# adaLN in a two-layer diffusion block: the context vector's products on GpSimd and ScalarE

## The chip, the core and the metric

One core of a Trainium2 chip runs the kernel. The metric is device microseconds of one execution, the median over the runs shown. The engines' names in the rows are PE (TensorE, matmuls), PEld (its weight loads), DVE (VectorE), ACT (ScalarE), POOL (GpSimd) and SP (SyncE, which issues transfers).

## The reference, cut to what matters

Two layers over 256 latent tokens `h` and 256 context tokens `hc`, D = 1024. In each layer: a SwiGLU half step, token mixing by four kinds of attention, a second SwiGLU half step. Each sub-layer's input is normalised and modulated; shifts, scales and gates come from two conditioning vectors through one matrix per layer (adaLN):

```python
s_c, s_cc = silu(c), silu(c_ctx)
for l in range(2):
    mod   = (s_c  @ w_ada[l] + b_ada[l]).reshape(B, 9, 1, D)   # latent tokens
    mod_c = (s_cc @ w_ada[l] + b_ada[l]).reshape(9, D)         # context tokens
    h  = h  + 0.5 * mod[:, 2] * swiglu(modulate(h,  norm_ffn1[l], mod[:, 0], mod[:, 1]), ...)
    hc = hc + 0.5 * mod_c[2]  * swiglu(modulate(hc, norm_ffn1[l], mod_c[0],  mod_c[1]), ...)
    ...                                  # token mixing, modulations 3, 4, gate 5
    h  = h  + 0.5 * mod[:, 8] * swiglu(modulate(h, norm_ffn2[l], mod[:, 6], mod[:, 7]), ...)
    if not last:
        ...                              # the same for hc, with mod_c[5] to mod_c[8]
return rmsnorm(h, final_norm)
```

In layer 1, the last one, `mod_c[5]` to `mod_c[8]` have no use.

## The kernel before, in words

Activations lie feature-major in SBUF: 128 features on the partitions, up to 512 tokens (256 latent, 256 context) along the free axis. Products are made in split precision: each weight block of 128x1024 is loaded by SyncE (`wraw`, L124, three buffers), ScalarE makes its high part `whi` (L127) and VectorE the rest `wlo` (L128), with five buffers each; `mm3` (L132 on) then issues three matmuls for each of 8 contraction tiles.

A SwiGLU phase (`ffn`) walks over 22 feature tiles in three chunks of 8, 8 and 6. For each tile a **pair** of weights (gate and up) makes two accumulations in PSUM (`pgu`; the pool has four banks, that is two pairs), and `activate` forms the activation: `sg` = silu on ScalarE (L357), `af` on VectorE (L358), its high part `ah` on ScalarE (L371), the rest `al` on VectorE (L372). At a chunk's end come the **down** products `pd`: eight output tiles, each contracting over the 8 (or 6) activations of the chunk, and the residual's update on VectorE (L336).

The first pair of modulations of layer 0 is formed by matmuls in the opening. All others, 128 **tiles** of 128 output features, are spread over three SwiGLU phases by `Jobs`: 48 in layer 0's first (modulations 2 to 7), 32 in its second (8, and 0 to 2 of layer 1), 48 in layer 1's first (3 to 8). A pair counts as two slots and a down tile as one; the tiles are due at even steps over the first 56 slots, so a pair brings one or two in the phases with 48 tiles and one in the phase with 32. `ada_tile` has SyncE load a tile of the matrix (`wa`, L295, two buffers), and VectorE multiplies it with the latent and with the context vector, each product summed along the row (L298):

```python
for v in range(2):
    junk = pool.tile([P, D], F32, name="junk", tag="junk", bufs=1)
    ins = nc.vector.scalar_tensor_tensor(junk, w, 1.0, sbc[:, v], op0=ALU.mult, op1=ALU.mult, accum_out=m[:, t, v:v + 1])
```

After the eight tiles of a modulation `ada_end` adds the bias and folds in gain or factor (L305 to L310).

Each engine takes its instructions in a fixed order, which a scheduler derives from the program when it is built; transfers of weights and of `wa` tiles are issued by SyncE in one order, too. An instruction whose operands are late holds up everything behind it on its engine.

Of the kernel before, what the change touches and what calls it, by code (L numbers as in the profile page):

```python
# [11 lines left out]
F32 = mybir.dt.float32  # L12
F32R = mybir.dt.float32r
# [6 lines left out]
P = 128  # L20
D = 1024
# [16 lines left out]
# feature-major column tiles of w_in  # L38
# [11 lines left out]
def body(nc, tc, es, a):  # L50
# [9 lines left out]
    # ---------------------------------------------------------------- constants and small parameters  # L60
# [24 lines left out]
    rope = con[:, 0:4 * S].rearrange("p (a b) -> p a b", a=4)                 # cos32 sin32 cos64 sin64  # L85
    gmask = con[:, 4 * S:5 * S].rearrange("p (a b) -> p a b", a=2)
    nmask = con[:, 5 * S:6 * S]
    rev = pers.tile([P, P], F32R, name="rev")                                 # turns the 64 query columns of a grid row
# [9 lines left out]
    def late_constants():  # L98
        """-lam per layer, on every partition; rev"""
# [18 lines left out]
    # ---------------------------------------------------------------- helpers  # L118
    def weights(src, shape):
        """load a [128, k, cols] block of a weight and split it"""  # L120
# [19 lines left out]
    def rsqrt_cols(ps, n, inv, eps, eng):  # L140
        """[128, n] sums in PSUM -> 1 / sqrt(sum * inv + eps) in SBUF"""
# [16 lines left out]
    def rms_cols(parts, ntok, dim, eps, heads=1, eng=nc.gpsimd, pin=False):  # L158
        """parts [128, ntok]: squares that add up over the feature tiles. -> rstd [128 tokens, token tiles x heads]"""
# [10 lines left out]
    def rms_rows(y, ntok, heads=1, pin=False):  # L170
        """-> PSUM [128, ntok] with rstd of the tokens (and of the head of each partition) on every partition"""
# [10 lines left out]
    class Stats:  # L182
        """squares of the residual stream, summed tile by tile as it is finished"""
# [5 lines left out]
        def add(self, k, hv):  # L189
# [4 lines left out]
            if n == 0:  # L194
                nc.scalar.activation(acc, src, AF.Square)
            else:
                sq = tp.tile([P, S], F32, name="sq", tag="nt", bufs=3)
                nc.scalar.activation(sq, src, AF.Square)
                if n == KD - 1 and (len(self.n) == 1 or hv == CTX):        # the last tile's squares stay by themselves
                    self.parts[hv].append(sq)  # L200
                else:
                    nc.vector.tensor_add(acc, acc, sq)
# [5 lines left out]
    class Norm:  # L208
        """rmsnorm, scale and shift of the residual stream into the split operands u, half by half and tile by tile"""
# [23 lines left out]
        def rest(self, stats, hv, between, eng=nc.gpsimd, rs=None):  # L233
            """the norm of a half, with other work between its parts"""
# [12 lines left out]
    def finish_phase(tail, stats, halves, nxt):  # L247
        """the last feature tiles of a phase for one half after the other; the norm behind the first half is woven into the second"""
# [15 lines left out]
    def first_products(nrm, stats, halves, group, between=None):  # L264
        """the first products [(weights, PSUM, halves)] of a phase, k by k behind the norm; the norm of the second half is woven in"""
# [14 lines left out]
    # ---------------------------------------------------------------- adaLN  # L280
# [10 lines left out]

    def ada_tile(l, i, t, pool, sbc, pin):
# [3 lines left out]
        for v in range(2):  # L296
            junk = pool.tile([P, D], F32, name="junk", tag="junk", bufs=1)
            ins = nc.vector.scalar_tensor_tensor(junk, w, 1.0, sbc[:, v], op0=ALU.mult, op1=ALU.mult, accum_out=m[:, t, v:v + 1])  # L298
            if pin:
                tc.keep_in_program_order(ins)  # L300

    def ada_end(l, i):
        """+ bias; scale -> gain * (1 + scale); gate of a half step -> 0.5 * gate"""
# [11 lines left out]
    class Jobs:  # L315
        """adaLN tiles spread over the first slots of a phase of 64"""
# [30 lines left out]
    SKEW = 5                              # last feature tiles of a phase, done for one half after the other  # L347

    # ---------------------------------------------------------------- SwiGLU half step
    def ffn(l, nrm, stats, gate, wgu, wd, halves, nxt, jobs, fp, opening=None):  # L350
        ntok = S * len(halves)

        def activate(pg, pu, rs=None):
# [5 lines left out]
            else:  # L359
                # one PSUM tile per half: sums still without rstd, the shift's product behind them  # L360
# [72 lines left out]
    # ---------------------------------------------------------------- token mixing  # L433
# [3 lines left out]
    def mix(l, nrm, stats, gate, qh, nxt, mp):  # L437
        u = nrm.u
        nq = S * len(qh)                  # tokens that ask
# [15 lines left out]
        def proj(tile_id, ntok):  # L455
            """feature-major projection of u by one column tile of w_in -> PSUM"""
# [6 lines left out]
        def rotate(dst, src, which, rows=(0, P)):  # L463
            """dst[:, lat] = rope(src[:, lat]); both in SBUF, dst may be src"""
# [18 lines left out]
        def vtok(src_list, width):  # L483
            """token-major projection of u: src_list = blocks of k tiles [128, nk, width] -> PSUM per token tile"""
# [46 lines left out]
        # ---- q, k, v of the heads. Q[hd], K[hd]: lists of (stationary, moving) operands whose products add up to the scores  # L531
        Q, K, V = {}, {}, {}

        # MLA: the parts by themselves
        ML = {}

        class LatentNorm:
            """rmsnorm of a low-rank projection (its feature tiles in PSUM), split"""
# [60 lines left out]
        # differential: the blocks of 32 partitions hold pairs of parts (q, k) along the contraction; (hi, hi) lies where the projection left it  # L599
# [25 lines left out]
        def diff_v():  # L625
            """v of the differential heads and the rotary key that the MLA heads share"""
# [20 lines left out]
        # heads of 64: q = [hi lo] against k = [hi hi] and [lo lo]  # L647
# [49 lines left out]
        # neighbourhood bias and mask: the query columns lie reversed in it, the product with rev turns them  # L697
# [16 lines left out]
        # ---- softmax units  # L714
        ORD = (0, 2, 1, 3)                # order of the GQA heads
# [485 lines left out]
```

## Time and profile before

| | |
|---|---|
| median of 3 runs | 2155.68 us (2154.09 to 2156.24) |
| span of the profiled execution | 2153.2 us |
| TensorE busy | 2107.4 us, 98% |
| VectorE busy | 1469.2 us, 68% |
| ScalarE busy | 911.8 us, 42% |
| GpSimd busy | 180.7 us, 8% |
| the 256 adaLN products on VectorE | 312.3 us |

TensorE's matmuls overlap, so its busy time says that there is always one under way, not that each runs at its peak. Busy time of the other engines is a sum over stages; where one of them matters is told by the waits and by the timeline.

### The profile page before, as it was taken

The page shows a single profiled execution, that of the slowest core. Times are in us where ns is not written, and L with a number is a line of the kernel's source. Part 1 is how long each engine was busy: PE and PEld are TensorE (multiplying, and loading weights), DVE is VectorE, ACT ScalarE, POOL GpSimd, SP SyncE. Part 2 cuts the span into 40 slices and gives each one's busy share as a digit, 9 for nine tenths or more (in the row PEclk, how much of TensorE's full clock was granted, in tenths as well). Part 3 has the DMA queues.
Part 4 walks back from the last instruction along what each step waited for, and adds up shares of the span by engine and source line. Part 5 has one row for each costly group of instructions (what it writes and reads, how often), then busy time and mean ns, then how long its engine had stood idle before and what let it go on. Part 6 is the DMA issues. An engine that isn't in the chain of part 4 may idle for free.

```text
span 2153.2 us, 31572 instructions
## 1 busy us (share of the span) xinstructions
PE 2107.4 (98%) x12130; PEld 1805.8 (84%) x12130; DVE 1469.2 (68%) x2639; ACT 911.8 (42%) x1456; POOL 180.7 (8%) x322
## 2 busy tenths in 40 slices
PE   7999999999999999999999999999999999999998
PEld 5888888987777877988888898888889888999998
DVE  6776767678767665566665558767667887787655
ACT  3422222467655563432222233222225776765443
POOL 0000000110012112100000010000002433120000
PEclk9999999999999999999999999999999999999999
DMA  8555554241232223245444336555542335355553
GB/s 331 173 178 178 177 176 150 69 121 47 66 100 73 88 66 118 92 157 156 140 154 150 105 118 203 179 176 186 165 127 90 105 106 138 128 168 171 192 183 102
DMA packets 95207, 301.52 MB, mean 140 GB/s; under 512 B 18640, under 2 KB 20048, under 8 KB 94672
## 3 DMA queue, kind: packets, MB, share of 16 engines
q1 hardware_dynamic: 92080, 295.10, 43.0%
q0 software_dynamic: 2688, 4.20, 1.0%
q8 instruction: 96, 1.57, 0.3%
q14 instruction: 55, 0.45, 0.1%
q10 hardware_dynamic: 288, 0.20, 0.0%
HBM read 294.21 MB, written 1.05 MB: 137 GB/s over the span
## 4 chain that ended last, share of the span: by engine, by line
PE 89%; DVE 5%; ACT 2%; issue 1%; POOL 1%; DMA 1%; SPq 0%; DVEq 0%; POOLq 0%; ACTq 0%
PE pgu L134 13%; PE pgu L137 13%; PE pgu L138 13%; PE pd L137 6%; PE pd L138 6%; PE pd L134 6%; PE pgt L134 4%; PE pgt L137 4%; PE pgt L138 4%; PE av L789 2%; PE pj L134 2%; PE pj L137 2%; PE pj L138 2%; PE psS L735 2%; PE tps L775 1%
## 5 line engine op out<-in xcount | busy, mean ns | idle before, releaser
L127 ACT CAST whi<-wraw 128x1024 fp32r<-128x1024 f32 (+2 forms) x414 | 423.1, 1024 | 993.8 <-PE pgu L137 434.7
L128 DVE TENSOR_TENSOR wlo<-wraw,whi 128x1024 fp32r<-128x1024 f32 (+2 forms) x414 | 495.2, 1197 | 160.6 <-ACT whi L127 141.5
L134 PE MATMUL pgu<-uh,whi 128*128 128x512 f32 (+1 forms) x1440 | 511.9, 357 | 1.4 <-ACT sg L357 0.9
L137 PE MATMUL pgu<-ul,whi 128*128 128x512 f32 (+1 forms) x1440 | 512.7, 356 | 0.6 <-DVE ul L230 0.4
L138 PE MATMUL pgu<-uh,wlo 128*128 128x512 f32 (+1 forms) x1440 | 512.2, 356 | 0.0
L298 DVE SCALAR_TENSOR_TENSOR junk<-wa,sbc 128x1024 f32<-128x1024 f32 x256 | 312.3, 1220 | 3.1
L134 PEld LDWEIGHTS pgu<-uh,whi 128*128 128x128 f32 x1440 | 271.1, 189 | 43.4 <-issue 2.5
L137 PEld LDWEIGHTS pgu<-ul,whi 128*128 128x128 f32 x1440 | 272.1, 189 | 39.4 <-DVE ul L230 1.1
L138 PEld LDWEIGHTS pgu<-uh,wlo 128*128 128x128 f32 x1440 | 272.1, 189 | 39.1 <-DVE wlo L128 0.3
L137 PE MATMUL pd<-al,whi 128*128 128x512 f32 (+1 forms) x794 | 273.4, 344 | 0.2 <-DVE al L372 0.2
L134 PE MATMUL pd<-ah,whi 128*128 128x512 f32 (+1 forms) x794 | 273.5, 345 | 0.0
L138 PE MATMUL pd<-ah,wlo 128*128 128x512 f32 (+1 forms) x794 | 273.1, 344 | 0.0
L134 PE MATMUL pgt<-uh,whi 128*128 128x512 f32 (+1 forms) x512 | 176.5, 345 | 0.4 <-ACT cacc L548 0.4
L358 DVE TENSOR_TENSOR af<-sg,pgu 128x512 f32<-128x512 f32 (+1 forms) x86 | 53.6, 625 | 179.5 <-PE pgu L138 179.5
L137 PE MATMUL pgt<-ul,whi 128*128 128x512 f32 (+1 forms) x512 | 174.1, 340 | 0.0
L138 PE MATMUL pgt<-uh,wlo 128*128 128x512 f32 (+1 forms) x512 | 173.8, 339 | 0.0
L137 PEld LDWEIGHTS pd<-al,whi 128*128 128x128 f32 x794 | 149.3, 188 | 20.9 <-DVE al L372 0.9
L134 PEld LDWEIGHTS pd<-ah,whi 128*128 128x128 f32 x794 | 149.2, 188 | 20.0
L138 PEld LDWEIGHTS pd<-ah,wlo 128*128 128x128 f32 x794 | 149.1, 188 | 19.9
L336 DVE SCALAR_TENSOR_TENSOR h<-pd,mod,h 128x256 f32<-128x256 f32 x168 | 76.4, 480 | 105.7 <-PE pd L138 105.3
L148 POOL TENSOR_TENSOR rq<-ry 128x2 f32<-128x2 f32 (+2 forms) x48 | 12.1, 252 | 1252.5 <-DVE ry L146 1241.6
L134 PEld LDWEIGHTS pgt<-uh,whi 128*128 128x128 f32 x512 | 97.6, 191 | 13.2 <-issue 3.3
(240 smaller groups left out, 3125.2 us busy)
## 6 DMA issues: line engine op xcount, KB each, us to landing
wraw<-wgu SPq DMA_DIRECT2D x176, 512.0 KB, 3.3
wa<-wada SPq DMA_DIRECT2D x128, 512.0 KB, 4.2
wraw<-wd SPq DMA_DIRECT2D x64, 512.0 KB, 3.6
wraw<-wgate SPq DMA_DIRECT2D x64, 512.0 KB, 3.3
wraw<-win SPq DMA_DIRECT2D x28, 512.0 KB, 3.3
wraw<-wd SPq DMA_DIRECT2D x32, 384.0 KB, 3.1
w<-wada SPq DMA_DIRECT2D x16, 512.0 KB, 8.0
wraw<-wbr SPq DMA_DIRECT2D x16, 512.0 KB, 3.3
```

The costliest lines, as they stand in the source:

```text
L127: nc.scalar.copy(hi[:, :n], raw[:, :n])
L128: nc.vector.tensor_sub(lo[:, :n], raw[:, :n], hi[:, :n])
L134: ins = nc.tensor.matmul(ps, lh, rh, start=start, stop=False)
L137: nc.tensor.matmul(ps, lh, rl, start=False, stop=False)
L138: nc.tensor.matmul(ps, ll, rh, start=False, stop=stop)
L148: eng.tensor_mul(q[:, :n], y[:, :n], y[:, :n])
L298: ins = nc.vector.scalar_tensor_tensor(junk, w, 1.0, sbc[:, v], op0=ALU.mult, op1=ALU.mult, accum_out=m[:, t, v:v + 1])
L336: nc.vector.scalar_tensor_tensor(h[k][:, hv[0]:hv[1]], ps[:, off:off + S], gate[:, k, v:v + 1], h[k][:, hv[0]:hv[1]], op0=ALU.mult, op1=AL ...
L358: nc.vector.tensor_mul(af[:, :ntok], sg[:, :ntok], pu[:, :ntok])
L735: nc.tensor.matmul(ps[:, :nk], q_[:, q0:q0 + P], k_[:, self.k0:T], start=z == 0, stop=z == len(qs) - 1 and not bias_mm)
L775: nc.tensor.transpose(tps[:, b], self.p[:, b * P:(b + 1) * P], ident)
L789: nc.tensor.matmul(av[un.qt * 64:(un.qt + 1) * 64], V[br](u0.k0 // P + b, hd), un.pT[:, b], start=b == 0, stop=b == kt - 1)
```

## The change

The latent vector's product stays on VectorE. The context vector's is made in two steps: GpSimd multiplies the tile in place, after VectorE has read it, and ScalarE passes over the result and sums it into the modulation's column. The tile's buffer is free for the next transfer once ScalarE is through. For modulations 5 to 8 of layer 1 the context vector's product isn't formed; `ada_end` copies the latent column in its place. The rest of the diff is comments.

```diff
+    def ada_vectors(l, i):
+
+        return 1 if l == DEPTH - 1 and i > 4 else 2
+
     def ada_tile(l, i, t, pool, sbc, pin):
         m = mods[(l, i)]
         w = pool.tile([P, D], F32, name="wa", tag="wa", bufs=2)
         nc.sync.dma_start(w, a["wada"][(l * NMOD + i - 2) * KD + t])
-        for v in range(2):
-            junk = pool.tile([P, D], F32, name="junk", tag="junk", bufs=1)
-            ins = nc.vector.scalar_tensor_tensor(junk, w, 1.0, sbc[:, v], op0=ALU.mult, op1=ALU.mult, accum_out=m[:, t, v:v + 1])
-            if pin:
-                tc.keep_in_program_order(ins)
+        junk = pool.tile([P, D], F32, name="junk", tag="junk", bufs=1)
+        ins = nc.vector.scalar_tensor_tensor(junk, w, 1.0, sbc[:, 0], op0=ALU.mult, op1=ALU.mult, accum_out=m[:, t, 0:1])
+        if pin:
+            tc.keep_in_program_order(ins)
+        if ada_vectors(l, i) == 2:
+            nc.gpsimd.tensor_mul(w, w, sbc[:, 1])
+            nc.scalar.activation(w, w, AF.Copy, accum_out=m[:, t, 1:2])
 
     def ada_end(l, i):
...
+        n = ada_vectors(l, i)
+        if n == 1:
+            nc.vector.tensor_copy(mods[(l, i)][:, :, 1:2], mods[(l, i)][:, :, 0:1])
```

In the changed kernel the product on VectorE is L301, GpSimd's L305, ScalarE's sum L306, and lines behind it stand 9 lower (`sg` L366, `af` L367, `ah` L380, `al` L381).

TensorE's order stays as it was. On ScalarE, between the last two pairs of the first chunk of layer 0's first phase (`ah_964` belongs to the seventh pair, `sg_1044` and `ah_1048` to the eighth; `whi_1177` and `whi_1216` are weights of down tiles), before:

```order
L371 CAST ah_964<-af_961 128x512
L127 CAST whi_1177<-wraw_1175 128x1024
L357 ACTIVATE sg_1044<-pgu_988 128x512
L127 CAST whi_1216<-wraw_1214 128x1024
L371 CAST ah_1048<-af_1045 128x512
L127 CAST whi_1255<-wraw_1253 128x1024
```

and in the changed kernel:

```order
L380 CAST ah_964<-af_961 128x512
L306 ACTIVATE wa_968,mod0_2_110<-wa_968 128x1024
L366 ACTIVATE sg_1044<-pgu_988 128x512
L306 ACTIVATE wa_974,mod0_2_110<-wa_974 128x1024
L127 CAST whi_1177<-wraw_1175 128x1024
L127 CAST whi_1216<-wraw_1214 128x1024
L380 CAST ah_1048<-af_1045 128x512
```

Two sums stand in the row now; the second is ahead of `whi_1177`, and both `whi` follow `sg_1044` directly.

On VectorE at the same place (`wa_968` and `wa_974` are adaLN tiles, `mod0_2` the modulation that they complete), before:

```order
L372 TENSOR_TENSOR al_965<-af_961,ah_964 128x512
L298 SCALAR_TENSOR_TENSOR junk_970,mod0_2_110<-wa_968,sbc_649 128x1024
L298 SCALAR_TENSOR_TENSOR junk_972,mod0_2_110<-wa_968,sbc_649 128x1024
L298 SCALAR_TENSOR_TENSOR junk_976,mod0_2_110<-wa_974,sbc_649 128x1024
L128 TENSOR_TENSOR wlo_1178<-wraw_1175,whi_1177 128x1024
L298 SCALAR_TENSOR_TENSOR junk_978,mod0_2_110<-wa_974,sbc_649 128x1024
L305 TENSOR_TENSOR mod0_2_110<-mod0_2_110,par_90 128x16
L310 TENSOR_SCALAR mod0_2_110<-mod0_2_110 128x16
L358 TENSOR_TENSOR af_1045<-sg_1044,pgu_995 128x512
L128 TENSOR_TENSOR wlo_1217<-wraw_1214,whi_1216 128x1024
L372 TENSOR_TENSOR al_1049<-af_1045,ah_1048 128x512
```

and in the changed kernel:

```order
L381 TENSOR_TENSOR al_965<-af_961,ah_964 128x512
L301 SCALAR_TENSOR_TENSOR junk_970,mod0_2_110<-wa_968,sbc_649 128x1024
L301 SCALAR_TENSOR_TENSOR junk_976,mod0_2_110<-wa_974,sbc_649 128x1024
L314 TENSOR_TENSOR mod0_2_110<-mod0_2_110,par_90 128x16
L319 TENSOR_SCALAR mod0_2_110<-mod0_2_110 128x16
L128 TENSOR_TENSOR wlo_1178<-wraw_1175,whi_1177 128x1024
L367 TENSOR_TENSOR af_1045<-sg_1044,pgu_995 128x512
L128 TENSOR_TENSOR wlo_1217<-wraw_1214,whi_1216 128x1024
L381 TENSOR_TENSOR al_1049<-af_1045,ah_1048 128x512
```

Two of the four products are gone, and `wlo_1178`, which needs `whi_1177`, stands behind the rest of them and the end of the modulation, still ahead of `af_1045`.

On SyncE's queue two pairs earlier (`wraw_905` is a weight of the seventh pair, `wraw_982` and `wraw_989` of the eighth; `wraw_1064` is the first down weight), before:

```order
L124 DMA wraw_905<-wgu1 128x1024
L295 DMA wa_734<-wada 128x1024
L124 DMA wraw_982<-wgu1 128x1024
L124 DMA wraw_989<-wgu1 128x1024
L295 DMA wa_810<-wada 128x1024
L124 DMA wraw_1064<-wd1 128x1024
L295 DMA wa_816<-wada 128x1024
```

and in the changed kernel:

```order
L124 DMA wraw_905<-wgu1 128x1024
L299 DMA wa_734<-wada 128x1024
L124 DMA wraw_982<-wgu1 128x1024
L124 DMA wraw_989<-wgu1 128x1024
L299 DMA wa_810<-wada 128x1024
L299 DMA wa_816<-wada 128x1024
L124 DMA wraw_1064<-wd1 128x1024
```

The two `wa` transfers stand side by side now, ahead of `wraw_1064`; `wraw_989` stands ahead of both, as it did.

## Rows read from the trace of the kernel before

**Rows 1.** The page: busy us of each engine, share of the span, instructions

```profile
PE 2107.4 (98%) x12130; PEld 1805.8 (84%) x12130; DVE 1469.2 (68%) x2639; ACT 911.8 (42%) x1456; POOL 180.7 (8%) x322
```

**Rows 2.** TensorE's waits: line, whom it waited for, total us, times, longest

```profile
PE pa L1002 <- DMA w<-wada: 12.4, 2, 12.2
...
PE pgu L134 <- ACT sg L357: 0.9, 2, 0.4
...
PE pgu L137 <- DVE ul L230: 0.4, 1, 0.4
...
PE pd L137 <- DVE al L372: 0.2, 1, 0.2
```

**Rows 3.** Busy us by stretch, inside the second SwiGLU phase's adaLN stretch

```profile
core 0: us, PE busy (x) PEld busy (x) DVE busy (x) ACT busy (x) POOL busy (x), PEclk, DMA share, GB/s
...
1300.00:1400.00 100.00, 100.00 (x437) 81.83 (x437) 78.24 (x119) 26.36 (x31) 0.00 (x0) 1.00 0.61 196
```

**Rows 4.** Groups by shape, VectorE then ScalarE: busy us, mean ns, idle before

```profile
L128 DVE TENSOR_TENSOR wlo<-wraw,whi 128x1024 fp32r<-128x1024 f32 x364 | 448.4, 1233 | 135.2 <-ACT whi L127 116.0 <-PE pgu L137 12.5
L298 DVE SCALAR_TENSOR_TENSOR junk<-wa,sbc 128x1024 f32<-128x1024 f32 x256 | 312.3, 1220 | 3.1
...
L127 ACT CAST whi<-wraw 128x1024 fp32r<-128x1024 f32 x364 | 382.0, 1051 | 878.0 <-PE pgu L137 370.8 <-PE pd L137 254.8 <-PE pgt L137 93.1
...
L755 ACT ACTIVATION_READ_ACCUMULATOR pexp<-psS,nm 128x1 f32 x120 | 23.7, 197 | 0.0
...
L510 ACT ACTIVATE sig<-sig 128x1024 f32<-128x1024 f32 x16 | 17.0, 1061 | 0.1
```

**Rows 5.** Line L529 on GpSimd, whole trace and 804 to 814: min/median/max ns

```profile
L529 POOL TENSOR_TENSOR merged<-merged,sig x48: 732/1294/2281, 652.4 to 1926.1; 128x512 f32<-128x512 f32 x24, 128x256 f32<-128x256 f32 x24
...
L529 POOL TENSOR_TENSOR merged<-merged,sig x4: 1285/1296/1300, 805.8 to 813.2; 128x512 f32<-128x512 f32 x4
```

**Rows 6.** Timeline at 835, VectorE and GpSimd: start us, us, instruction

```profile
835.70 1.60 DVE L128 TENSOR_TENSOR wlo<-wraw,whi 128x1024 fp32r<-128x1024 f32 x1 [0.16 <-ACT whi L127]
...
834.93 3.52 POOL L529 TENSOR_TENSOR merged<-merged,sig 128x512 f32<-128x512 f32 x2 [20.40 <-DVE sig L528]
```

**Rows 7.** Timeline of VectorE, last two pairs of the first chunk

```profile
111.60 0.69 DVE L358 TENSOR_TENSOR af<-sg,pgu 128x512 f32<-128x512 f32 x1 [3.38 <-PE pgu L138]
...
113.54 0.68 DVE L372 TENSOR_TENSOR al<-af,ah 128x512 fp32r<-128x512 f32 x1
114.14 1.22 DVE L298 SCALAR_TENSOR_TENSOR junk<-wa,sbc 128x1024 f32<-128x1024 f32 x1
...
115.40 1.23 DVE L298 SCALAR_TENSOR_TENSOR junk<-wa,sbc 128x1024 f32<-128x1024 f32 x1
...
122.48 0.69 DVE L358 TENSOR_TENSOR af<-sg,pgu 128x512 f32<-128x512 f32 x1 [1.82 <-PE pgu L138]
123.28 1.23 DVE L128 TENSOR_TENSOR wlo<-wraw,whi 128x1024 fp32r<-128x1024 f32 x1
124.42 0.68 DVE L372 TENSOR_TENSOR al<-af,ah 128x512 fp32r<-128x512 f32 x1
```

**Rows 8.** Timeline of ScalarE, the same place

```profile
117.75 0.59 ACT L357 ACTIVATE sg<-pgu 128x512 f32<-128x512 f32 x1
122.19 1.06 ACT L127 CAST whi<-wraw 128x1024 fp32r<-128x1024 f32 x1 [3.85 <-PE pgu L137]
123.20 0.62 ACT L371 CAST ah<-af 128x512 fp32r<-128x512 f32 x1
```

**Rows 9.** ScalarE's waits, of all engines' waits

```profile
ACT whi L127 <- PE pgu L137: 434.7, 122, 5.7
```

**Rows 10.** Timeline of TensorE, the first down product of the first chunk

```profile
122.21 0.40 PE L134 MATMUL pd<-ah,whi 128*128 128x512 f32 x1
...
127.34 0.40 PE L137 MATMUL pd<-al,whi 128*128 128x512 f32 x1
```

**Rows 11.** Tile wa: its transfers' us from issue to landing

```profile
DMA to landing us min/median/max: 3.1/4.2/8.4
```

## The prediction

> **What bounds the kernel now.** I began with the busy line of the page: TensorE is busy 98% of the span, VectorE 68%, ScalarE 42%, GpSimd 8% [rows 1]. Then I asked what TensorE itself waits for [rows 2]: the longest entry is a weight transfer in the opening, and in the SwiGLU phases, where all adaLN tiles lie, there are only entries under 1 us in total, such as `al` of VectorE with 0.2. The table by stretches says the same: from 1300 to 1400 us, in the middle of an adaLN stretch, TensorE is busy 100.00 of 100 us, with VectorE at 78.24 [rows 3]. So VectorE's adaLN products are hidden already. Taking them away can give back almost nothing; the question is only whether the new way of forming them reaches TensorE.
>
> **What leaves and what comes.** 128 tiles were multiplied twice on VectorE, 256 products of 1.22 us [rows 4]. Now 128 remain; 96 of the others move (layer 1 leaves out 32: modulations 5 to 8), so VectorE loses 128 x 1.26 = 161 us (1.26 is the distance from one product to the next, 114.14 to 115.40 [rows 7]). This is worth 0 to 1.5 us of the span: TensorE's waits for ScalarE and VectorE in those phases, 0.9 + 0.4 + 0.2 [rows 2]. I take 0. The `tensor_copy` that `ada_end` gains in layer 1 is 128x8, on an engine with that much freed; I count nothing for it.
>
> The moved product has no row. GpSimd's 128x512 addition takes 1.30 us when left alone, the 128x256 one 0.73 at least [rows 5]; the difference, 0.57 per 256 columns, gives 1.30 + 2 x 0.57 = 2.4 us for 128x1024. Bounds: VectorE's own 1.26 below, four narrow instructions, 2.9, above. I take 2.4, since it continues the two rows of the same operation. In the Trainium skill, "GPSIMD Engine Reference", section 3.1, a two-input addition of 2048 elements is given as 4497 ns; half of it would be 2.25, an estimate that would lower the sum below by about 4 us. No run here has that size. The section 4.1 of the same page advises against this kind of move (elementwise work on VectorE, GpSimd about twice as slow); the sum below says where that would be felt.
>
> ScalarE's sum: a pass over 128x1024 takes 1.06 us and reading an accumulator 0.20 [rows 4], together 1.26. 96 of these are 121 us on an engine that is idle more than half the time; by load alone nothing happens.
>
> GpSimd and VectorE also exclude each other. At 835.70 a `wlo` of VectorE takes 1.60 us, where its mean is 1.23, and ends at 837.30; the two GpSimd additions begun at 834.93 take 3.52 us instead of 2.6 [rows 6]. One ran, then the other, then the first again. So a GpSimd product cannot run beside a VectorE product of two SBUF operands.
>
> **The wait that the change adds.** ScalarE works in order. In the new order a sum stands ahead of `whi` (a weight's high part), and behind `whi` come `wlo`, `af`, `al` on VectorE, and behind `al` the next tiles' products. That closes a loop over one pair of up weights. For a pair with two tiles, counted from the start of `al`: first product at 0.6 (113.54 to 114.14), second at 1.9, done at 3.2 [rows 7]; GpSimd's two products behind it, each excluded while VectorE multiplies, until 3.1 + 2 x 2.4 = 7.9; the second sum 1.26, 9.2; `whi` 1.05, 10.2; `wlo` 1.14 (123.28 to 124.42), 11.4; `af` 0.69, 12.1; the other `wlo` 1.14; next `al` at **13.2**. TensorE needs 10.9 for a pair (`af` at 111.60 and 122.48 [rows 7]). Each such pair falls behind by 2.3 us. With one tile: product done at 1.9, GpSimd 4.3, sum 5.6, `sg` 0.59 [rows 8], `whi` 7.2, `wlo` 8.4, `af` 9.1, `al` at **10.2**: it recovers 0.7 us. Where an `ada_end` stands between two tiles, VectorE waits there for a sum before the second product: 5.7, product to 7.2, GpSimd 9.6, sum 10.9, `whi`, `wlo`, `al` at 13.1, or 14.3 if a `wlo` gets ahead of GpSimd; I take +2.8. Before, none of this was in the path: `whi` and `al` waited for TensorE alone [rows 8].
>
> Within a chunk a lag costs nothing. Weights are split about one and a half pairs ahead, so a lag of 12 us leaves some 5 us; ScalarE's `whi` now waits for TensorE 434.7 us in 122 times [rows 9]. The accumulators have four banks, two pairs. The first place without cover is a chunk's end, where the down products contract over the activations just made. The first down product starts at 122.21 and meets the last `al` at its 23rd matmul, 127.34 [rows 10]; `al` was done at 124.42 + 0.68 = 125.1 [rows 7]. So 2.2 us of lag are free; in the third chunk, with six activations instead of eight, 6 matmuls of 0.233 less: 0.8 us. What exceeds this is lost one to one, as TensorE has nothing else to do.
>
> Going through the new order pair by pair:
> - Layer 0, first FFN, chunk 1: double, double, single, double: 2.3 + 2.3 - 0.7 + 2.3 = 6.2. Here a transfer comes on top: SyncE issues tile `wa_810` only behind a weight transfer that waits for the pair's first `wlo`; with 4.2 us from issue to landing [rows 11] the next product starts 5.9 us after that `wlo` began, not 3.5. Loop by loop this makes 2.6, 4.7, 1.7 and 2.4, together 11.4. Minus 2.2: **9.2** (4.0 without the transfer's part).
> - Chunk 2: double, double, single, split by an `ada_end`, double, double: 2.3 + 2.3 - 0.7 + 2.8 + 2.3 + 2.3, and 0.5 for a transfer: 11.8. Minus 2.2: **9.6**.
> - Chunk 3: 2.3 + 2.8 - 0.7, then two pairs whose first `whi` stands between the two sums, 12.0 each, +1.1 and +1.1: 6.6. Minus 0.8: **5.8**.
> - Layer 1, first FFN, chunk 1: a late third tile of the first pairs, +4.4, then 1.8 - 0.7 + 2.3 + 2.3 - 0.7: 9.4. Minus 2.2: **7.2**. From chunk 2 on layer 1 forms one vector only: nothing.
> - Layer 0, second FFN: 32 tiles over the same slots, one per pair, one split pair, which four singles work off: **0**.
>
> Down stretches hold fewer than one tile per weight and the lag is worked off there. The sum is 31.8 us. The profiled execution spans 2153.2 us against a median of 2155.7 of the three runs, so 2.5 us lie around it or between executions: 2153.2 + 31.8 + 2.5 = **2187 us**. With 2.9 us per GpSimd product a double pair takes 14.2 and a single 10.7; the same lists give 12, 15, 9, 11 and 1, together 48: 2204. With 1.26 a double takes 10.9, no lag; the split pairs and the transfers leave about 5: 2161.
>
> **Rivals.**
> 1. No change. If GpSimd's product is about as fast as VectorE's, or if lags stay below the free 2.2 us, TensorE sees nothing: 2154 to 2160. For it: 98% busy, and no entry above 0.9 us in these phases. Against: GpSimd's rows, by which a double pair exceeds TensorE's 10.9 by a fifth.
> 2. Faster. The 161 us taken from VectorE shorten the way from the last accumulation to `al` at chunk ends. The point from which it decides is a chunk end at which TensorE waits for VectorE now; only 0.2 us of that is there, and the whole list for these phases is 1.5: 2154.2, not beyond 0.2%.
> 3. Slower still. Every GpSimd product meets a VectorE instruction and takes 2.9 or more, singles no longer recover, the second FFN of layer 0 begins to lag too, and weights come late inside chunk 2: 2204 to 2225. Rows 6 speak for it (3.52 for 2.6); against it, in a double pair VectorE has nothing to do while GpSimd multiplies, since its next `wlo` waits for the sum.
>
> **How the numbers follow.** Forecast (2167 to 2204) 57%; slower still 17%; little more than nothing, 2160 to 2167, 6%; no change 16%; faster by more than 0.2%, 4% (something in the order that I don't see). 0.2%, about 4.3 us, is what a measurement of this kernel can tell from no change. Faster 0.04, same 0.16, slower 0.80. The range 2156 to 2210 leaves out the faster cases, half of no change and the upper part of the third rival, not quite 2 in 10; the forecast's own is 2167 to 2204.
>
> **What the profile after would show.** L305 on GpSimd near 2.4 us, x96; L306 on ScalarE 1.06; waits of `whi` for GpSimd's sums in place of waits for TensorE; VectorE's busy time near 1310 us; TensorE idle 4 to 10 us, on `al` (L381) or `ah` (L380), some 5 us behind the start of the first down product of the four chunks named and nowhere in the second FFN of layer 0. If GpSimd's product is right and TensorE still doesn't wait, the free lag at chunk ends is wrong; if it waits in the middle of chunks, for weights or accumulators, the cover is.

## The result, and the profile after

The changed kernel takes **2181.3 us** (median of 4 runs, 2180.58 to 2181.75) against 2155.1 (4 runs, 2154.09 to 2156.24): ratio 1.012, 95% interval 1.0108 to 1.0133. It is slower, by 26 us; 2187 was forecast. The profiled execution spans 2180.0 us, before 2153.2.

The page's busy line, beside [rows 1]:

```profile
PE 2117.1 (97%) x12130; PEld 1811.7 (83%) x12130; DVE 1348.0 (62%) x2387; ACT 1011.1 (46%) x1648; POOL 445.9 (20%) x418
```

VectorE has lost 121 us and GpSimd has gained 265, ScalarE 99. TensorE does the same 12130 matmuls and is still 97% busy; the loss is in a few places. Its list of waits tells which (line, whom it waited for, total us, times, longest):

```profile
PE pd L134 <- ACT ah L380: 16.0, 4, 6.2
PE pa L1011 <- DMA w<-wada: 11.9, 2, 11.7
...
PE pd L137 <- DVE al L381: 1.6, 4, 0.6
```

The opening's wait is as it was [rows 2]. New are four waits of the down products for `ah`, each with a short one for `al` behind it. They lie at 126.87 (1.4 us), 262.64 (6.1), 380.19 (2.3) and 1383.97 (6.2): the ends of the three chunks of layer 0's first FFN and of the first chunk of layer 1's. The second FFN of layer 0 has none.

The moved work: GpSimd's product (L305), ScalarE's sum (L306), and ScalarE's groups by shape (busy us, mean ns, idle before):

```profile
L305 POOL TENSOR_TENSOR wa<-wa,sbc x96: 2357/2404/3447, 71.7 to 1410.1; 128x1024 f32<-128x1024 f32 x96
```

```profile
L306 ACT ACTIVATE wa<-wa x96: 1056/1062/1066, 74.1 to 1412.5; 128x1024 f32<-128x1024 f32 x96
```

```profile
L127 ACT CAST whi<-wraw 128x1024 fp32r<-128x1024 f32 x364 | 378.9, 1047 | 464.7 <-PE pgu L137 138.8 <-PE pd L137 110.3 <-PE pgt L137 92.4
L306 ACT ACTIVATE wa<-wa 128x1024 f32<-128x1024 f32 x96 | 101.9, 1061 | 363.1 <-POOL wa L305 363.1
```

A product takes 2.36 to 2.40 us left alone (median 2404 ns) and up to 3.45 where it meets VectorE, as 42 of the 96 do; the mean is 2.78. Before, `whi` had 370.8 us of idle time ended by TensorE's up products [rows 4]; of that 138.8 are left, and 363.1 us of waiting for GpSimd have come in their place. That is the wait that the change adds, on an engine that is busy 46%.

One turn of the loop, in the last pair of the first chunk, on VectorE, GpSimd and ScalarE (start us, us, instruction, idle before it and what ended it), to be read beside [rows 7, 8]:

```profile
115.88 0.69 DVE L381 TENSOR_TENSOR al<-af,ah 128x512 fp32r<-128x512 f32 x1
116.48 1.22 DVE L301 SCALAR_TENSOR_TENSOR junk<-wa,sbc 128x1024 f32<-128x1024 f32 x1
...
117.74 1.23 DVE L301 SCALAR_TENSOR_TENSOR junk<-wa,sbc 128x1024 f32<-128x1024 f32 x1
...
124.79 0.18 DVE L314 TENSOR_TENSOR mod<-mod,par 128x16 f32<-128x16 f32 x1 [5.82 <-ACT wa L306]
...
125.73 1.23 DVE L128 TENSOR_TENSOR wlo<-wraw,whi 128x1024 fp32r<-128x1024 f32 x1 [0.55 <-ACT whi L127]
126.87 0.68 DVE L367 TENSOR_TENSOR af<-sg,pgu 128x512 f32<-128x512 f32 x1
127.47 1.22 DVE L128 TENSOR_TENSOR wlo<-wraw,whi 128x1024 fp32r<-128x1024 f32 x1
128.60 0.68 DVE L381 TENSOR_TENSOR al<-af,ah 128x512 fp32r<-128x512 f32 x1
```

```profile
117.84 5.74 POOL L305 TENSOR_TENSOR wa<-wa,sbc 128x1024 f32<-128x1024 f32 x2 [7.47 <-DVE junk L301]
```

```profile
123.61 1.06 ACT L306 ACTIVATE wa<-wa 128x1024 f32<-128x1024 f32 x1 [0.72 <-POOL wa L305]
124.57 0.18 ACT L306 ACTIVATION_READ_ACCUMULATOR wa<-wa 128x1 f32 x1
124.67 1.98 ACT L127 CAST whi<-wraw 128x1024 fp32r<-128x1024 f32 x2
```

From `al` at 115.88 the chain runs over the two products, GpSimd's two (done at 123.58), the second sum, `whi`, `wlo`, `af` and `wlo` to `al` at 128.60: 12.72 us, where TensorE needs 10.9. VectorE stands still for 5.82 us in it. The relieved engine is idle, and waits for the engine that relieved it.

### The profile page after: what moved, and what is told of

Read it like the earlier page. It is cut to its first block, busy times and chain, and to the rows that moved or that the text cites. A ratio compares the mean times of both kernels' runs of the same rounds, so it can differ in the third digit from the quotient of the medians.

```text
span 2180.0 us, 31596 instructions
## 1 busy us (share of the span) xinstructions
PE 2117.1 (97%) x12130; PEld 1811.7 (83%) x12130; DVE 1348.0 (62%) x2387; ACT 1011.1 (46%) x1648; POOL 445.9 (20%) x418
## 5 line engine op out<-in xcount | busy, mean ns | idle before, releaser
L128 DVE TENSOR_TENSOR wlo<-wraw,whi 128x1024 fp32r<-128x1024 f32 (+2 forms) x414 | 514.2, 1244 | 362.7 <-ACT whi L127 346.6
L305 POOL TENSOR_TENSOR wa<-wa,sbc 128x1024 f32<-128x1024 f32 x96 | 266.6, 2782 | 554.5 <-DVE junk L301 476.2
L134 PE MATMUL pd<-ah,whi 128*128 128x512 f32 (+1 forms) x794 | 277.9, 350 | 16.0 <-ACT ah L380 16.0
L137 PE MATMUL pd<-al,whi 128*128 128x512 f32 (+1 forms) x794 | 277.9, 350 | 1.6 <-DVE al L381 1.6
L306 ACT ACTIVATE wa<-wa 128x1024 f32<-128x1024 f32 x96 | 101.9, 1061 | 363.1 <-POOL wa L305 363.1
L301 DVE SCALAR_TENSOR_TENSOR junk<-wa,sbc 128x1024 f32<-128x1024 f32 x128 | 168.1, 1313 | 6.8 <-DMA wa<-wada 6.1
L538 POOL TENSOR_TENSOR merged<-merged,sig 128x512 f32<-128x512 f32 (+1 forms) x48 | 61.6, 1303 | 243.1 <-DVE sig L537 213.8
```

Source lines behind the costliest of these rows:

```text
L128: nc.vector.tensor_sub(lo[:, :n], raw[:, :n], hi[:, :n])
L134: ins = nc.tensor.matmul(ps, lh, rh, start=start, stop=False)
L137: nc.tensor.matmul(ps, lh, rl, start=False, stop=False)
L301: ins = nc.vector.scalar_tensor_tensor(junk, w, 1.0, sbc[:, 0], op0=ALU.mult, op1=ALU.mult, accum_out=m[:, t, 0:1])
L305: nc.gpsimd.tensor_mul(w, w, sbc[:, 1])
L306: nc.scalar.activation(w, w, AF.Copy, accum_out=m[:, t, 1:2])
```

## A second loss behind the stalls: TensorE's clock

The stretches around the long waits (us, busy time of each engine, granted clock, DMA) show more than idle time, beside a stretch of the same kernel right behind:

```profile
core 0: us, PE busy (x) PEld busy (x) DVE busy (x) ACT busy (x) POOL busy (x), PEclk, DMA share, GB/s
262.00:274.00 12.00, 5.65 (x14) 3.82 (x13) 7.65 (x9) 5.61 (x9) 4.40 (x2) 0.72 0.55 175
274.00:286.00 12.00, 12.00 (x53) 9.71 (x53) 7.46 (x12) 5.68 (x9) 5.67 (x2) 1.00 0.52 182
1383.00:1397.00 14.00, 7.48 (x20) 5.24 (x19) 6.73 (x10) 5.24 (x9) 6.53 (x3) 0.63 0.43 143
```

```profile
130.60:133.90 3.30, 3.30 (x9) 2.57 (x8) 1.89 (x4) 0.00 (x0) 3.30 (x2) 0.50 0.42 151
```

The granted clock falls to 0.50, the 1.2 GHz level of the two, and stays there when the products run again. One sees it in TensorE's timeline behind the first wait too: matmuls that started every 0.23 us start every 0.43.

```profile
130.15 0.39 PE L137 MATMUL pd<-al,whi 128*128 128x512 f32 x1
130.38 0.48 PE L138 MATMUL pd<-ah,wlo 128*128 128x512 f32 x1
130.66 0.63 PE L134 MATMUL pd<-ah,whi 128*128 128x512 f32 x1
131.08 0.63 PE L137 MATMUL pd<-al,whi 128*128 128x512 f32 x1
```

The kernel before has no such stretch in these places. The ends of the two chunks with the long waits lie at 254 to 266 and 1360 to 1374 in it (same columns):

```profile
254.00:266.00 12.00, 12.00 (x53) 9.64 (x53) 9.73 (x16) 3.43 (x4) 0.00 (x0) 1.00 0.56 174
1360.00:1374.00 14.00, 14.00 (x62) 11.27 (x61) 13.65 (x23) 3.59 (x4) 0.00 (x0) 1.00 0.54 167
```

The prediction had none either. The Trainium skill, "TensorE: Matmul & The Clock Gate", Part 1, says that the gate halves the clock after TensorE has been idle; the trace agrees behind the two long waits, 6.1 and 6.2 us, with 0.50. Behind the short ones, 1.4 and 2.3 us, this trace has 0.50 too, but the run with filled stalls, below, has the same first wait and no fall.

Since both kernels issue the same matmuls in the same order in these phases, the loss by place can be read from when the same matmul starts in each trace. "Lag" is how far the pair loop fell behind over the chunk; the free part is taken off, 2.2 us, in the third chunk 1.3. The prediction had 0.8 there. In the trace of the kernel before, the third chunk's last `al` is done at 366.57 and first used at 367.87:

```profile
365.89 0.68 DVE L372 TENSOR_TENSOR al<-af,ah 128x512 fp32r<-128x512 f32 x1
367.87 0.40 PE L137 MATMUL pd<-al,whi 128*128 128x512 f32 x1
```

| chunk end | forecast | lag less free | moved in all | remainder |
|---|---|---|---|---|
| layer 0 first FFN, chunk 1 | 9.2 | 4.6 - 2.2 = 2.4 | 3.9 | 1.5 |
| chunk 2 | 9.6 | 9.3 - 2.2 = 7.1 | 8.9 | 1.8 |
| chunk 3 | 5.8 | 4.4 - 1.3 = 3.1 | 4.8 | 1.7 |
| layer 1 first FFN, chunk 1 | 7.2 | 9.4 - 2.2 = 7.2 | 9.7 | 2.5 |
| sum | 31.8 | 19.8 | 27.3 | 7.5 |

The remainder is what the lower clock costs, by this account; one experiment below tests it. The rest of the span's difference of 26.8 is small and of both signs: one more short fall at a phase boundary, at 1284 (1.5 us), and none at 1828, where the kernel before has one (1.5 us).

## The experiments

My theory: a sum that waits for GpSimd stands ahead of `whi` in ScalarE's order; so GpSimd's duration comes into the pair loop once for each tile, and the lag is paid at chunk ends. Rivals: the sum's 1.26 us on ScalarE are too much; VectorE and GpSimd exclude each other, and that is the price wherever the sum stands; the transfers of `wa` come late.

**The sums one pair later.** Same work on the same engines. The sums move in ScalarE's order, the end of a modulation moves with them, and four buffers hold the products until then (the next run has the four buffers alone).

```diff
+        def flush(self):
+            for l, i, t, w in self.late:
+                if ada_vectors(l, i) == 2:
+                    tc.keep_in_program_order(nc.scalar.activation(w, w, AF.Copy, accum_out=mods[(l, i)][:, t, 1:2]))
+                if t == KD - 1:
+                    ada_end(l, i)
+            self.late = []
...
-                ada_tile(l, i, t, self.pool, self.sbc, self.n < PIN)
+                self.late.append((l, i, t, ada_tile(l, i, t, self.pool, self.sbc, self.n < PIN)))
```

> Change: the sums of the context products are issued one pair of products later, behind the next pair's ah in ScalarE's order, so that none of them waits for GpSimd; four buffers wa instead of two carry the products until then. Work, engines and tile counts are those of the changed kernel. Theory (the sum stands ahead of whi in ScalarE's order and makes whi, wlo and the next pair wait for GpSimd): the pairs with two tiles fall from 12.7 us to about 10.9 to 11.3, TensorE's waits for ah at the four chunk ends shrink from 16.0 us to under 3, the falls of the granted clock go with them, 2155 to 2162 us. Rival (the exclusion of VectorE and GpSimd is the price, wherever the sum stands): pairs with two tiles stay at 12 us or more, 2172 to 2181. Rival (the 1.26 us of ScalarE are the price): the same 2172 to 2181, since all of it is still there.

Measured: 2156.32 us against 2156.45, ratio 1.0 (0.9991 to 1.0009). The whole loss is gone. TensorE has no wait for `ah` or `al` any more. The product on GpSimd, and the same pair on VectorE:

```profile
L305 POOL TENSOR_TENSOR wa<-wa,sbc x96: 2391/3262/3448, 72.3 to 1380.6; 128x1024 f32<-128x1024 f32 x96
```

```profile
113.31 0.69 DVE L388 TENSOR_TENSOR al<-af,ah 128x512 fp32r<-128x512 f32 x1
...
117.61 2.13 DVE L128 TENSOR_TENSOR wlo<-wraw,whi 128x1024 fp32r<-128x1024 f32 x1 [1.21 <-ACT whi L127]
122.26 0.69 DVE L374 TENSOR_TENSOR af<-sg,pgu 128x512 f32<-128x512 f32 x1 [2.52 <-PE pgu L138]
...
124.19 0.69 DVE L388 TENSOR_TENSOR al<-af,ah 128x512 fp32r<-128x512 f32 x1
```

`al` to `al` is 10.88 us, TensorE's pace, and `af` waits for TensorE again. GpSimd and VectorE now meet more often than in the changed kernel: the median product takes 3.26 us instead of 2.40, and this `wlo` 2.13 instead of 1.2. It costs nothing. So neither their exclusion nor ScalarE's load is the price, but the place of the sums. ScalarE's waits for GpSimd have not vanished (35 times, 107.5 us), yet where they stand nobody is late:

```profile
ACT whi L127 <- PE pgu L137: 310.5, 95, 5.7
ACT wa L334 <- POOL wa L305: 107.5, 35, 5.7
```

**Four buffers alone**, which the kernel above also needs:

```diff
-        w = pool.tile([P, D], F32, name="wa", tag="wa", bufs=2)
+        w = pool.tile([P, D], F32, name="wa", tag="wa", bufs=4)
...
-    W0 = [("w0", 4)] * 4 + [("wa", 2)] * 2 + [("junk", 1)]
+    W0 = [("w0", 2)] * 2 + [("wa", 4)] * 4 + [("junk", 1)]
```

> Change: the changed kernel with four buffers wa instead of two (the opening's buffers are dealt out anew for it), nothing else. It is also the control for the run in which the sums are issued later. Theory: the transfers are in good time already and the loop runs through the engines' orders, so 2178 to 2184 us and pairs with two tiles at 12.7 us. Rival (a buffer that comes free late, or its transfer, holds the product back): the pairs get shorter and the time falls below 2175.

Measured: 2181.5 us, ratio 1.0116 (1.0099 to 1.0133): the changed kernel's time, with its waits (the one in layer 1 is 5.5 us instead of 6.2, as the first pairs there fell 0.8 us less behind).

```profile
PE pd L134 <- ACT ah L380: 15.1, 4, 6.1
PE pd L137 <- DVE al L381: 1.2, 3, 0.6
```

So buffers and their transfers are not the cause but for that 0.8 us, and the gain of the kernel above is not theirs.

**The product on VectorE, the sum left on ScalarE.**

```diff
-            nc.gpsimd.tensor_mul(w, w, sbc[:, 1])
+            nc.vector.tensor_mul(w, w, sbc[:, 1])
```

> Change: the product of the context vector goes back to VectorE (a plain product, about 1.2 us by the rows of the same shape), the sum stays on ScalarE, GpSimd does nothing for it. Theory (the wait for GpSimd's 2.4 us ahead of whi is the price): pairs with two tiles take about 10.9 to 11.3 us, the four stalls all but vanish, 2155 to 2163 us, though VectorE now has as much work as in the kernel before. Rival (the sum's 1.26 us on ScalarE in itself is the price): pairs with two tiles stay over 12 us, 2170 to 2181. Rival (VectorE was the bound and the relief helps): over 2181, since the relief is taken back and the sum stays.

Measured: 2155.1 us, ratio 0.9995 (0.9986 to 1.0005). The product now stands in this row:

```profile
L305 DVE TENSOR_TENSOR wa<-wa,sbc x96: 1216/1224/1227, 71.9 to 1380.4; 128x1024 f32<-128x1024 f32 x96
```

VectorE is busy 1432.9 us again and TensorE does not wait. The sum's 1.26 us are harmless; 2.4 us for the product instead of 1.2 were what the loop could not hold. One reservation: by the changed cost the scheduler set one `whi` between the two sums, so the order of ScalarE is not quite that of the changed kernel.

**GpSimd's step at several lengths.** 512, 640 or 896 of the 1024 columns. With 512 the scheduler sets a `whi` between the sums here too; with 640 and 896 ScalarE's order in these chunks is that of the changed kernel, so that only the duration differs.

```diff
-            nc.gpsimd.tensor_mul(w, w, sbc[:, 1])
+            nc.gpsimd.tensor_mul(w[:, :640], w[:, :640], sbc[:, 1, :640])
```

> Change: GpSimd multiplies 512 of the 1024 columns and leaves the rest of the context vector's products out; the sum on ScalarE keeps its size. So this is the changed kernel with GpSimd's step at about 1.3 us instead of 2.4. Theory (a loop in which GpSimd's duration counts once for each tile): a pair with two tiles falls by up to 2 x 1.1 us, to TensorE's own 10.9, no stall is left, 2155 to 2159 us. Rival (ScalarE's sum is the price): 2172 to 2181.

> Change: GpSimd multiplies 640 of the 1024 columns and leaves the rest of the context vector's products out. Unlike with 512 columns, where the scheduler also set one whi between the two sums, ScalarE's order stays that of the changed kernel; so only the duration of GpSimd's step differs, about 1.57 us instead of 2.40 (between the 1.30 of 512 columns and the 2.40 of 1024). Theory (the duration counts once for each tile in the loop): a pair with two tiles takes 12.73 - 2 x 0.83 = 11.1 us, one with a single tile waits for TensorE, the split pair 12.1; no chunk ends over its free lag, 2154 to 2158 us. Rival (the gain with 512 columns came from the other order of whi and sums, not from the shorter step): 2170 to 2181.

> Change: the same with 896 columns, GpSimd's step at about 2.13 us, ScalarE's order that of the changed kernel. Theory: a pair with two tiles 12.73 - 2 x 0.27 = 12.2 us, a single 9.6, the split pair 13.2; lags over the free ones of 0.4, 4.1, 1.1 and 1.8 us at the four chunk ends, 7.4 in all, and 2 to 4 us for the clock behind them: 2163 to 2168 us. Rival (a stall appears or not, whatever the size of the step): 2178 to 2182 or 2154 to 2158.

GpSimd's product in the runs with 640 and 896 columns:

```profile
L305 POOL TENSOR_TENSOR wa<-wa,sbc x96: 1557/1576/2648, 72.2 to 1382.2; 128x640 f32<-128x640 f32 x96
```

```profile
L305 POOL TENSOR_TENSOR wa<-wa,sbc x96: 2098/2128/3177, 71.6 to 1395.2; 128x896 f32<-128x896 f32 x96
```

| columns | product, median us | pair with two tiles | split pair | time | ratio, 95% interval |
|---|---|---|---|---|---|
| 512 | 1.30 | 10.88 (TensorE's) | 11.6 | 2155.0 | 0.9992 (0.9983 to 1.0002) |
| 640 | 1.58 | 11.08 | 12.12 | 2154.94 | 0.9994 (0.9984 to 1.0003) |
| 896 | 2.13 | 12.18 | 13.24 | 2169.14 | 1.0059 (1.0044 to 1.0074) |
| 1024 | 2.40 | 12.73 | 13.79 | 2181.3 | 1.012 (1.0108 to 1.0133) |

From 640 to 1024 columns the product grows by 0.82 us and the pair by 1.65, twice as much: once for each of its two tiles, as the loop says. With 640 a pair is already over TensorE's 10.88, yet no lag passes the free 2.2 us and the time stays. With 896 it is paid mostly at two places, by waits of 3.1 and 3.2 us (the other two chunk ends lose 0.5 and 0.8 us, with no fall of the clock); the time came out 1 us above the expected 2163 to 2168, since the first pairs of layer 1 fell further behind (5.7 us) than I had counted (4.0).

**GpSimd's step doubled.**

```diff
             nc.gpsimd.tensor_mul(w, w, sbc[:, 1])
+            nc.gpsimd.tensor_mul(w, w, sbc[:, 1])
```

> Change: the changed kernel with GpSimd's product made twice (the values are then no longer the reference's context vector's products), so about 4.8 us of GpSimd for each tile; the scheduler also puts the first whi ahead of the first sum. Theory (a loop that holds one GpSimd step for each tile): by the chain sum after sum a pair with two tiles takes about 16.2 us, 5.3 more than TensorE's 10.9, one with one tile about 10.8. The four chunks lose about 14, 25, 26 and 24 us, the second FFN of the first layer about 3, and the clock 10 to 15: 2240 to 2275 us. Rival (GpSimd runs beside the rest and only its exclusion of VectorE counts): a pair with two tiles 13 to 14 us, 2195 to 2215. Rival (GpSimd's time does not matter once the stalls are there): 2181 to 2190.

Measured: 2316.23 us, ratio 1.0742 (1.0726 to 1.0758): 160 us lost, where I had expected 84 to 119. The direction holds and the rivals fall, but the size was off. The two products of a tile, and TensorE's waits:

```profile
L305 POOL TENSOR_TENSOR wa<-wa,sbc x96: 2345/3202/3391, 74.6 to 1556.3; 128x1024 f32<-128x1024 f32 x96
L306 POOL TENSOR_TENSOR wa<-wa,sbc x96: 2339/2406/3282, 77.1 to 1558.8; 128x1024 f32<-128x1024 f32 x96
```

```profile
PE pd L134 <- ACT ah L381: 72.9, 9, 14.5
PE pgu L134 <- ACT sg L367: 29.4, 12, 7.3
PE pd L134 <- ACT sg L367: 14.3, 5, 6.7
```

A tile costs GpSimd 5.6 us, not 4.8, because the first of the two meets VectorE. A pair with two tiles takes 16.8 us (16.2 expected), and one with a single tile 11.5 instead of 10.8, which is over TensorE's 10.9: singles no longer recover. So the second FFN of layer 0, made of singles, lost about 31 us (I had expected 3), and the lag outgrew its cover: waits for `sg`, which holds the accumulators, appear inside the chunks. This is the prediction's third rival, at a price that the changed kernel doesn't reach.

**The halves of the change.** Only the unused modulations left out; then only the move, for all 128 tiles.

```diff
-            nc.gpsimd.tensor_mul(w, w, sbc[:, 1])
-            nc.scalar.activation(w, w, AF.Copy, accum_out=m[:, t, 1:2])
+            junk = pool.tile([P, D], F32, name="junk", tag="junk", bufs=1)
+            ins = nc.vector.scalar_tensor_tensor(junk, w, 1.0, sbc[:, 1], op0=ALU.mult, op1=ALU.mult, accum_out=m[:, t, 1:2])
+            if pin:
+                tc.keep_in_program_order(ins)
```

> Change: only the second half of the change: the unused context modulations are not formed, all other products and sums stay on VectorE as in the kernel before. Theory (VectorE is not the bound anywhere in these stages): 2153 to 2157 us, no difference from the kernel before. Rival (less work on VectorE shortens something): below 2151.

```diff
-        return 1 if l == DEPTH - 1 and i > 4 else 2
+        return 2
```

> Change: only the first half of the change: the context products of all 128 tiles go to GpSimd and ScalarE, none is left out. Theory (each chunk whose pairs carry two moved tiles falls behind by about 1.8 us per such pair less the free 2.2 at its end): the chunks 2 and 3 of the last layer's first FFN, which the changed kernel spares, now stall as well, by some 7 and 4 us and the clock's 1 to 3 us for each, 2192 to 2200 us. Rival (the stalls come from something else in those four places): 2179 to 2184.

Measured: 2154.73 us for the first, ratio 0.9995 (0.9986 to 1.0004): 32 products less on VectorE give nothing. The second takes 2187.92, ratio 1.0146 (1.0131 to 1.0162), below the 2192 to 2200 expected. TensorE's waits in it:

```profile
PE pd L134 <- ACT ah L380: 21.1, 5, 6.2
PE pd L137 <- DVE al L381: 1.9, 5, 0.6
```

One more stall, not two. The end of chunk 2 in layer 1 loses 7.7 us, clock included; chunk 3 there ends with two pairs of one tile each, which worked the lag off (8.6 and 9.2 us a pair). I had taken it for a copy of layer 0's chunk 3, which ends with doubles. So leaving out the unused modulations, which is worth nothing by itself, spares the moved version some 6 us (2187.92 against 2181.3; the four runs of the first lie between 2184.66 and 2190.08).

**More cover at the chunk's end.** The first two down products interleaved, those on the last activation at the end; in the changed kernel and, as a control, in the kernel before.

```diff
+                if m == 0:
+                    ws = [weights(a[wd][l, q, :, j0:j1, :], [P, nk, P]) for q in range(2)]
+                    two = {q: psmm.tile([P, 512], F32, name="pd", tag="mm") for q in range(2)}
+                    for ks in (range(nk - 1), range(nk - 1, nk)):
+                        for q in range(2):
+                            for k in ks:
+                                mm3(two[q][:, :ntok], wk(ws[q], k), (act[k][0][:, :ntok], act[k][1][:, :ntok]), k == 0, k == nk - 1)
...
```

> Change: the changed kernel, with the first two down products of each chunk interleaved: all products of both on the earlier activations first, those on the last activation of the chunk at the end. The end of a chunk so has about 4.9 us more (3.5 in the third) before TensorE needs the last ah and al. Theory (the loop falls behind TensorE in steps and is paid for at a chunk's end alone): stalls of about 0, 2, 0 and 2 us instead of 2.3, 7.1, 3.6 and 7.2, with shorter falls of the clock behind them, 2158 to 2168 us, while pairs with two tiles keep their 12.7. Rival (the stalls are not paid at the end of a chunk but in every pair): 2178 to 2184.

> Change: the kernel before with the same interleaved down products, as the control. Theory: it had no wait at the ends of these chunks, so the interleaving gives nothing, 2153 to 2158 us. Rival (the interleaving is good or bad in itself): outside of 2151 to 2160.

Measured: 2163.18 us for the changed kernel with it, ratio 1.0035 (1.0022 to 1.0047), and 2154.69 for the kernel before with it, 0.9994 (0.9985 to 1.0004). In the first:

```profile
PE pd L134 <- ACT ah L380: 4.4, 2, 3.0
```

Two of the four stalls are gone and the others are 3.0 and 1.4 us, while pairs with two tiles still take 12.7. So the lag is paid at the chunk's end and nowhere else; 18 of the 26 us come back without touching the loop.

**TensorE kept busy in the stalls.** The lag stays; 24 products that nobody reads fill the two long waits.

```diff
+                    if m == 0 and k == nk - 1 and wgu == "wgu1" and (l, c) in ((0, 1), (1, 0)):
+                        fill = psmm.tile([P, 512], F32, name="pfill", tag="mm")
+                        for _ in range(8):
+                            mm3(fill[:, :hi - lo], wk(w_, 0), (act[0][0][:, lo:hi], act[0][1][:, lo:hi]), True, True)
```

> Change: the changed kernel with 24 extra products of 128x512 (24 x 0.233 = 5.6 us, results never read) just ahead of the last activation's products in the first down product of the two chunks with the long stalls (TensorE's waits of 6.06 and 6.22 us). The loop, and with it the moment at which the last ah and al are there, stays as it is; only what TensorE does meanwhile differs. Theory (the granted clock falls to half because TensorE has stood still, and that is 1.5 to 2.4 and 2.1 to 2.9 us of the loss at these two places): the remaining waits are under 1 us each, no fall of the clock follows them, and the time comes out shorter though TensorE does more, 2175.5 to 2178 us. Rival (the lower clock at these places doesn't come from the stall): 2180.5 to 2183. Rival (the extra products themselves delay something): over 2184.

Measured: 2178.06 us (2176.17 to 2178.88), ratio 1.0103 (1.0086 to 1.012). That is at the upper edge of what was expected, and the interval overlaps with the changed kernel's, so the time alone would not decide. The trace does. The same two stretches (same columns):

```profile
262.00:274.00 12.00, 10.86 (x46) 8.25 (x45) 8.33 (x10) 5.52 (x9) 3.79 (x3) 1.00 0.55 175
1379.00:1393.00 14.00, 12.74 (x54) 9.79 (x53) 6.73 (x10) 5.29 (x8) 6.53 (x3) 1.00 0.41 135
```

The clock stays at 1.00, and what follows moves by 7.15 us at the first place and 7.28 at the second, where it was 8.9 and 9.7. These are the lags less the free 2.2 (9.35 and 9.48 in this run), with no remainder. The first chunk of this run adds a comparison that the edit didn't intend. Its lag of 4.6 us and its waits, 1.4 us for `ah` and 0.6 for `al`, are those of the changed kernel, but the clock stayed up behind them:

```profile
130.90:134.20 3.30, 3.30 (x16) 2.66 (x15) 1.86 (x4) 0.00 (x0) 3.30 (x2) 1.00 0.42 140
```

What follows moved by 2.5 us there instead of 3.9, the lag less the free 2.2 and next to nothing more. So the remainder in the table is the clock, as three of the four places show, and at the two long stalls the clock fell because TensorE stood still. Why one stall of 1.4 us is followed by a fall and another like it is not stays open. It also means that the gain in time is not all the edit's in every run: in the profiled execution, the fastest of the four, 4.2 us come from the two filled places and 1.4 from the first chunk.

## Why the prediction came out right, step by step

- **VectorE's relief is worth nothing**: right. It lost 121 us (161 were forecast as removed, to near 1310 us, and it stands at 1348.0; longer instructions that met GpSimd took some back). Neither the run with 32 products less nor the one with VectorE's work put back differs in time from the kernel before.
- **GpSimd's product, 2.4 us**: right, 2404 ns as the median. The Trainium skill's figure in "GPSIMD Engine Reference", section 3.1, halved, gave 2.25; the trace has 2.36 at the least. What that estimate would take off the sum, put at 4 us, is 5 by the prediction's own slope (48 instead of 31.8 us of lag for 0.5 us of product). The advice of the page's section 4.1 held here: no run with the whole product on GpSimd was faster than the kernel before.
- **The sum on ScalarE, 1.26 us and harmless by load**: right, though one sum follows another instruction by 1.06, since reading the accumulator overlaps (123.61 to 124.67).
- **The loop**: right as a mechanism, shown by the sums moved by one pair and by the lengths of GpSimd's step. The periods of doubles and singles were 0.3 to 0.5 us too long, 12.73 for 13.2 and 9.87 for 10.2; the split pair, taken at 10.9 + 2.8, was right with 13.79. By steps: GpSimd done 7.70 us after `al` (7.9 forecast), `whi` begun at 8.79 (9.2), `wlo` at 9.85 (10.2), `af` at 10.99 (11.4). GpSimd 0.2 us earlier, the sum's reading 0.2 and an `af` that hands over after 0.60 instead of 0.69 are the difference. Over the pairs of the second chunk that is 2 us. In the third chunk the two pairs forecast at 12.0 took 11.0 and 11.3. Layer 1's lag came out at the forecast 9.4 by luck: its third pair fell behind by 2.6 instead of 1.8, doubles by 1.9 instead of 2.3.
- **The free lag**: 2.2 us is right; in the run with filled stalls lag and loss differ by just that. The 0.8 us of the third chunk should have been 1.3: besides the 6 matmuls less, its last `al` starts only 1.7 us behind the first down product (364.15 to 365.89), not 2.2. With 896 columns, where no fall of the clock blurs it, the chunk had a lag of 2.0 and lost 0.8.
- **The places**: right, all four, 5.1 us behind the start of the first down product at the first (some 5 forecast), and none in layer 0's second FFN. The idle times with the short wait for `al`, 2.0, 6.3, 2.8 and 6.5 us, are under the forecast 4 to 10 at two of them.
- **The late transfer in chunk 1, 5.2 us**: wrong in its mechanism. The prediction had tile `wa_810` held up by the weight transfer ahead of it. That one, `wraw_989`, was issued at 80.65, 6.4 us before the tile. What the tile waited for is its buffer: the first sum, from 85.91 to 87.07 with its reading, frees it, and SyncE issues it at 87.09; `wa_816` follows behind the second sum, and the weights behind both:

```profile
87.09 2.69 SPq L299 DMA_DIRECT2D wa<-wada  x2
91.65 2.06 SPq L124 DMA_DIRECT2D wraw<-wd  x2
```

The first product that needs them starts at 93.87, right behind `al`. Landing got quicker too:

```profile
DMA to landing us min/median/max: 3.1/3.3/7.1
```

Why was not tried, but it did not decide: with the 4.2 us of [rows 11] both tiles would have been there in time. The first chunk ran at 12.73 like the others and lost 2.4 us to lag, not 9.2.
- **The clock**: not foreseen. I took a stall's price for its length. The four stalls cost over a third more, 7.5 on top of 19.8.

So the forecast of 2187 was 5.7 us high by two errors of opposite sign: the sum of lags 12.0 too large (5.7 of it transfers, 5.8 periods, 0.5 the free lag of the third chunk), the clock's 7.5 left out. The remaining 1.2 lie in the small places and in the 2.5 us added for what is outside the span, which were 1.8 in the profiled execution. Its reason was right. That its sum was better than its terms is luck.

## What to carry over

Before moving work to an idle engine, follow the in-order queue of every engine that it passes: a short step that waits for the slow engine holds up all that is queued behind it, and two engines busy 20 and 46% of the time can set the pace between them. If the work fits by load, move the step that waits behind the step that is urgent; here that, with the buffers that it needs, turned 1.2% slower into no change. And this kernel, whose TensorE is 98% busy and waits for VectorE next to nowhere, had nothing to win from relieving VectorE; such a move is worth making only where a wait for that engine shows.

## What the hardware showed

A stall of TensorE costs more than its length. Behind waits of 1.4 to 6.2 us the granted clock stood at 0.50, and matmuls came every 0.43 us instead of 0.23; that was 1.5 to 2.5 us each by the table. Short waits have either outcome: the wait of 1.4 us that the interleaved kernel keeps was followed by no fall, nor was the first one of the run with filled stalls, the same as the changed kernel's. With 24 unread products of 0.23 us in a 6-us wait the clock stayed at 1.00, and the kernel was not slower for the extra work, though it did more.

VectorE and GpSimd exclude each other for whole instructions, and the one that comes second waits. In the changed kernel a product begun at 145.43, 0.2 us behind a `wlo` of 1.22, took 3.26 us instead of 2.40; a `wlo` begun at 150.84, 0.3 us behind a product of 2.40, took 3.19 instead of 1.23. In the run with later sums that happened to most products (median 3.26), and alone it cost nothing.
